# Expert weights of a mixture-of-experts layer kept in fp32, multiplied in halves and quarters of the TensorE array

## The chip, the cores and the metric

The kernel runs on one core of one Trainium2 chip. The metric is device time in microseconds for one launch. TensorE does the matrix products, VectorE (DVE), ScalarE (ACT) and GpSimd (POOL) the elementwise work, SyncE (SP) issues the transfers.

## The reference, cut to what matters

A two-layer decoder trunk on 272 tokens of width 1024 (16 of them learned ones that are dropped at the end). Each layer mixes tokens with three branches; layer 0 then has a dense SwiGLU, layer 1 the expert layer that the change touches:

```python
logits = xt @ router_w                       # 256 tokens x 8 experts
top_v, top_i = lax.top_k(logits, 2)
comb = sum(one_hot(top_i) * softmax(top_v))  # weight of each expert for each token
for e in range(8):                           # D_FF_EXPERT = 3584
    out = out + comb[:, e:e+1] * (silu(xt @ wg[e]) * (xt @ wu[e])) @ wd[e]
```

All tensors are float32.

## The kernel before, in words

All weights lie in one array `w` of units of 128 x 2048 float32 (1 MB). The dense part takes 109 units, each expert 42. `Stream` loads the units in order into a ring of tiles (names `raw`, and later `xh`, `xl`, `lt`, `mg`, which the dense part has freed). A tile that is released lets SP issue the next load. `Stream.block(512)` hands out the next 512 columns; an expert has 168 such blocks of 128 x 512 (256 KB each): for each of 7 slices `j` of the hidden width, 8 blocks for the gate and 8 for the up product (`gate_up`), then 8 blocks for the product with the down weights of slice `j-1` (`down`).

The tokens of an expert are gathered into slots with one-hot matrices (`Run.gather`). The experts are worked on in the order q = 0 to 7, of the kinds `KINDS = "BSBSBBBS"`, ordered by load so that an S expert has at most 64 tokens and a B expert at most 96 (`SMALL`, `CAP`). A general version for fuller experts stands behind a condition (`tc.If`) and isn't executed with these inputs.

A B expert works on split weights. `Stream.high` copies half a unit to fp32r on ACT (`whi`, L152), `Stream.low` subtracts on DVE (`wlo`, L165), and `mm3` makes three fp32r products of 512 columns for each block (L275 to L277), with 96 slots as the stationary operand and the activations split too (`xgh`, `xgl`, and `eh`, `el` for the hidden values). An S expert takes the weights as they are, in fp32 (`st.whole`): for each block two products of 256 columns, with the 64 slots in the left and in the right 64 columns of the array (L1309, L1328), which write partitions 0 to 63 and 64 to 127 of one PSUM bank. The trace shows each fp32 product as two MATMULs.

Hidden values are brought to the other layout by TensorE transposes (`transpose_h` L1208, `transpose_small` L1214), and each expert's results go back to the tokens by products with the one-hot matrix (`scatter` L1231, `scatter_small` L1238) and an accumulation on DVE. Much of that is put into `pending`, from which `gate_up` takes one piece before k = 3 and k = 6 of each product. A helper `keep_clock` multiplies junk in halves and in quarters of the array during the routing (L306).

Experts are gathered in groups, (0), (1, 2), (3, 4), (5, 6, 7); at the end of a group (`turnover`) the next one is gathered, and `slot_rms` (L1113, L1114) brings the norm's scale to the slots. Expert 0 runs alone: behind it all pending work is done at once, all engines load a flag, and experts 1 to 7 stand inside `tc.If(full <= CAP)`.

Of the kernel before, what the change touches and what calls it, by code (L numbers as in the profile page):

```python
# [16 lines left out]
P = 128  # L17
# [17 lines left out]
PASSES = -(-SEQ // CAP)  # L35
SMALL = 64

# [10 lines left out]
UNITS = DENSE_UNITS + NEXP * EXP_UNITS  # L48

# [30 lines left out]
class Stream:  # L80
# [5 lines left out]
    def __init__(self, nc, w, raws, hl, nhl, first, last):  # L86
        self.nc, self.w = nc, w
        self.ring = list(raws)
        self.at = 0
        self.hl, self.nhl = hl, nhl  # L90
        self.next_dma, self.end = first, last
        self.next_hi = self.next_lo = 2 * first
        self.cur = 2 * first - 1
        self.units, self.halves = {}, {}
        self.pos, self.first = 0, 2 * first
        self.whole, self.src = set(), lambda u: w[u]
        self.used, self.oldest, self.apart = set(), first, set()
# [45 lines left out]
    def high(self):  # L143
# [12 lines left out]
    def low(self):  # L156
        h = self.next_lo
        if h // 2 in self.whole:
            self.next_lo += 1
            if h % 2:  # L160
                del self.units[h // 2]
            return
# [15 lines left out]
    def advance(self):  # L178

        if self.cur < self.pos // HALF + self.first:  # L180
            self.halves.pop(self.cur, None)
            if self.cur % 2 and self.cur // 2 in self.whole:
                self.release(self.cur // 2)
# [19 lines left out]
def _build(ctx, tc, nc, A, out, dbg):  # L203
    V, S, G, PE = nc.vector, nc.scalar, nc.gpsimd, nc.tensor
    w = A["w"]
    NRAW, NHL, NRAWB, NRAWC = 6, 3, 4, 1
# [693 lines left out]
    def before_last():  # L900
# [11 lines left out]
        slots2 = me.tile([P, 2 * SMALL], F32, name="slots2")  # L912
# [7 lines left out]
        G.iota(slots2, pattern=[[0, 2], [1, SMALL]], base=1, channel_multiplier=0, allow_small_or_imprecise_dtypes=True)  # L920
        G.iota(index, pattern=[[1, NEXP]], base=0, channel_multiplier=0, allow_small_or_imprecise_dtypes=True)
        for k_, v_ in (("tri", tri), ("oneb", oneb), ("lower", lower), ("slots", slots), ("slots2", slots2),
# [59 lines left out]
    tri, oneb, lower, slots, slots2 = em["tri"], em["oneb"], em["lower"], em["slots"], em["slots2"]  # L982
# [24 lines left out]
    es = me.tile([P, 512], F32, name="es")  # L1007
# [27 lines left out]
    tiles = {}  # L1035

    def kept(pool, shape, dt, nm):

        if nm not in tiles:
            tiles[nm] = pool.tile(shape, dt, name=nm)  # L1040
        return tiles[nm]

    class Run:


        def __init__(self, kinds, groups, pos, comb):
            self.kinds, self.groups, self.pos, self.comb = kinds, groups, pos, comb
            self.x, self.oh, self.at, self.turn = {}, {}, {}, 0
# [5 lines left out]
        def first(self, i):  # L1054

            return SMALL if any(self.small(q) for q in self.groups[i]) else 0

        def onehot(self, i):
            oh = [kept(me, [P, 2 * SMALL + 2 * CAP], F32R, f"oh{t}") for t in range(2)]
            o = 0  # L1060
            for q in sorted(self.groups[i], key=lambda q: not self.small(q)):
                n = 2 * SMALL if self.small(q) else CAP
                self.at[q] = o
                for t in range(2):
                    V.tensor_scalar(oh[t][:, o:o + n], slots2 if self.small(q) else slots, self.pos[:, t, q:q + 1], None,
                                    op0=OP.is_equal)
                self.oh[q] = [oh[t][:, o:o + n] for t in range(2)]
                o += n
            self.all = [oh[t][:, self.first(i):o] for t in range(2)]

        def gather(self, i, c2, tag):

            if c2 == 0:
                for q in self.groups[i]:
                    if self.small(q):
                        self.x[q] = kept(mo, [P, KD, SMALL], F32, "xn")
                    else:
                        self.turn = 1 - self.turn
                        self.x[q] = [kept(mo, [P, KD, CAP], F32R, f"{n}{self.turn}") for n in ("xgh", "xgl")]
            p = bank(tag)  # L1080
            n = self.all[0].shape[1]
            for c in range(2):
                cc = 2 * c2 + c
                for k, src in enumerate((em["nh"], em["nl"])):
                    for t in range(2):
                        PE.matmul(p[:, c * n:(c + 1) * n], lhsT=src[:, t, cc * P:(cc + 1) * P], rhs=self.all[t],
                                  start=k + t == 0, stop=k + t == 2)

            def part(q, c):
                o = c * n + (0 if self.small(q) else self.at[q] - self.first(i))  # L1090
                return p[:, o:o + (SMALL if self.small(q) else CAP)], pp("g_ffn", 1, 1, 2 * c2 + c)

            for q in self.groups[i]:
                for c in range(2):
                    src, g = part(q, c)
                    if self.small(q):
                        V.tensor_scalar(self.x[q][:, 2 * c2 + c, :], src, g, None, op0=OP.mult)
                    else:
                        S.activation(self.x[q][0][:, 2 * c2 + c, :], src, AF.Copy, scale=g)
            for q in self.groups[i]:  # L1100
                if not self.small(q):
                    for c in range(2):
                        src, g = part(q, c)
                        h, l = (x[:, 2 * c2 + c, :] for x in self.x[q])
                        V.scalar_tensor_tensor(l, src, g, h.bitcast(F32), op0=OP.mult, op1=OP.subtract)

        def slot_rms(self, i):

            p = bank("o")
            for q in self.groups[i]:  # L1110
                n = self.oh[q][0].shape[1]
                for t in range(2):
                    PE.matmul(p[:n, q:q + 1], lhsT=self.oh[q][t].bitcast(F32), rhs=ssq[:, t:t + 1], start=t == 0, stop=t == 1)  # L1113
                V.tensor_copy(rs[:n, q:q + 1], p[:n, q:q + 1])  # L1114

    def again_by_tokens(t, d):
# [5 lines left out]
        split_to(em["nh"][:, t, cs], em["nl"][:, t, cs], acc[t][d])  # L1122
# [4 lines left out]
    rs = one([P, NEXP], F32, "rs")  # L1127
# [3 lines left out]
    V.tensor_reduce(cnt, pp_[:, 16:24], axis=AX.X, op=OP.max)  # L1131
# [23 lines left out]
    S.activation(rs[:, :2], ssq, AF.Silu)  # L1155
# [12 lines left out]
    flag = one([P, 1], F32, "flag")  # L1168
    flagi = one([P, 1], I32, "flagi")
    sq = [P, NEXP, NEXP]  # L1170

    def rank_steps():

        a, b = pair_
        V.tensor_scalar(cn[:, 0:1], cn[:, 0:1], 2.0 * SEQ, None, op0=OP.add)
        cj, ce = cn[:, None, :].to_broadcast(sq), cn[:, :, None].to_broadcast(sq)
# [18 lines left out]
        V.tensor_tensor(b[:, 0], a[:, 1], cn, op=OP.mult)  # L1195
        V.tensor_reduce(flag, b[:, 0], axis=AX.X, op=OP.add)
        V.scalar_tensor_tensor(flag, flag, float(CAP - SMALL), cnt, op0=OP.add, op1=OP.max)
        V.tensor_copy(flagi, flag)
# [3 lines left out]
    def room(name):  # L1202
        return mo.tile([P, 512], F32R, name=name, bufs=2)

    def transpose_h(h, dst):
        p = bank("acc")
        for b in range(4):
            PE.transpose(p[:, b * CAP:(b + 1) * CAP], h[:CAP, b * P:(b + 1) * P], ident[:CAP, :CAP])  # L1208
        split_to(*dst, p[:, :4 * CAP])

    def transpose_small(h, dst):
        p = bank("acc")
        for b in range(2):
            PE.transpose(p[:, b * P:(b + 1) * P], h[:, b * P:(b + 1) * P], ident)  # L1214
        V.tensor_copy(dst, p[:, :256])  # L1215

    def slots_by_token(run, q, oht):
        p = bank("o")
        n = run.oh[q][0].shape[1]
        for t in range(2):  # L1220
            PE.transpose(p[:n, t * P:(t + 1) * P], run.oh[q][t].bitcast(F32), ident)
        S.activation(oht[:n], p[:n, :256], AF.Copy)

    def split_y(ys, y):
        ys += [room(n) for n in ("eh", "el")]
        split_to(*(x[:CAP] for x in ys), y[:CAP])

    def scatter(run, q, oht, ys, t, d, tag):
        p = bank(tag)
        for i in range(2):  # L1230
            PE.matmul(p, lhsT=oht[:CAP, t * P:(t + 1) * P], rhs=ys[i][:CAP], start=i == 0, stop=i == 1)  # L1231
        V.scalar_tensor_tensor(acc[t][d], p, run.comb[:, t, q:q + 1], acc[t][d], op0=OP.mult, op1=OP.add)

    def scatter_small(run, q, oht, y, t, g, ds, tag):

        p = bank(tag)
        r = slice(g * SMALL, (g + 1) * SMALL)
        PE.matmul(p[:, :256 * len(ds)], lhsT=oht[r, t * P:(t + 1) * P].bitcast(F32),  # L1238
                  rhs=y[r, ds[0] * 256:(ds[-1] + 1) * 256], start=True, stop=True)
        for i, d in enumerate(ds):  # L1240
            o = acc[t][d][:, g * 256:(g + 1) * 256]
            V.scalar_tensor_tensor(o, p[:, i * 256:(i + 1) * 256], run.comb[:, t, q:q + 1], o, op0=OP.mult, op1=OP.add)
# [12 lines left out]
    def square_sums(d):  # L1255

        fin = XG["fin"]
        for t in range(2):
            scratch = me.tile([P, 512], F32, name="es")
# [22 lines left out]
    def experts(st, run, qs):  # L1282
# [3 lines left out]
        def hidden(q, j):  # L1286

            h = hid.get((q, j), ())
            if len(h) == 1:
                if run.small(q):  # L1290
                    h.append(room("eh")[:, :256].bitcast(F32))
                    transpose_small(h[0], h[1])
                else:
                    h += [room(n)[:, :4 * CAP] for n in ("eh", "el")]
                    transpose_h(h[0], h[1:])

        def gate_up(q, j, last):
            gu = []
            for m in range(2):
                a = bank(("acc", "s")[m])  # L1300
                for k in range(KD):
# [4 lines left out]
                    wh, wl = st.block(512)  # L1306
                    if run.small(q):
                        for g in range(2):
                            PE.matmul(a[g * SMALL:(g + 1) * SMALL, :256], lhsT=run.x[q][:, k, :],  # L1309
# [281 lines left out]
```

## Time and profile before

| | us |
|---|---|
| median of 3 runs (lowest, highest) | 1668.86 (1667.41, 1669.78) |
| the profiled execution, its own time | 1667.66 |
| span of its trace, first to last instruction | 1665.9 |
| first matmul of the experts, from the span's start | 758.06 |
| matmuls of B expert 0 | 758.1 to 883.8 |
| S expert 1 | 896.8 to 975.0 |
| B expert 2 | 975.0 to 1110.9 |
| S expert 3 | 1110.9 to 1191.0 |
| B experts 4, 5 and 6 | 1191.0 to 1568.4 |
| S expert 7 and the end | 1568.4 to 1665.9 |

The profile is of one execution. The matmul rows give the modelled time of a MATMUL from its start to its last result; matmuls follow each other sooner than that, so prices are read from start to start. Weight loads into the array have rows of their own (PEld).

### The profile page before, as it was taken

The numbers are of one execution on the slowest core, as the hardware profiler recorded it, in microseconds if no ns is written. First come the engines' busy times: TensorE is split into PE (matmuls) and PEld (weight loads), VectorE is DVE, ScalarE is ACT, GpSimd is POOL, SyncE is SP. The second block draws the span as 40 slices with busy tenths as digits, with TensorE's granted clock in tenths as the row PEclk, the third lists the DMA queues.
The fourth block names the chain that finished last, engine by engine and source line by source line (L and its number), as shares of the span: only waits on it lengthen the run. The fifth ranks groups of instructions, "written<-read, shape, count | busy, mean of one in ns | idle before, by whom it ended". The sixth has DMA issues, their size and how long they took to land.

```text
span 1665.9 us, 27719 instructions
## 1 busy us (share of the span) xinstructions
PE 1631.3 (98%) x10760; PEld 1319.1 (79%) x10760; DVE 1093.5 (66%) x1521; ACT 906.3 (54%) x1227; POOL 136.4 (8%) x205
## 2 busy tenths in 40 slices
PE   8999999999999999999998999999999999999997
PEld 8999999999999999997765656666666677777664
DVE  5667676555566576769993058950489898998602
ACT  5545656444444457557871048730377677778401
POOL 3301242000011002510000000000000000000000
PEclk9999999999999999998998999999999999999998
DMA  7333454544544336577895999999999999999994
GB/s 295 127 127 137 163 180 154 180 175 177 177 167 150 127 136 258 191 279 293 320 370 224 418 419 420 419 381 417 419 420 419 400 352 377 355 366 365 354 420 201
DMA packets 66235, 471.85 MB, mean 283 GB/s; under 512 B 7344, under 2 KB 7472, under 8 KB 9520
## 3 DMA queue, kind: packets, MB, share of 16 engines
q1 hardware_dynamic: 65952, 469.86, 72.5%
q8 instruction: 86, 1.41, 0.3%
q14 instruction: 53, 0.43, 0.1%
q10 hardware_dynamic: 144, 0.15, 0.0%
HBM read 468.93 MB, written 1.05 MB: 282 GB/s over the span
## 4 chain that ended last, share of the span: by engine, by line
PE 92%; DMA 3%; DVE 2%; POOL 1%; ACT 1%; issue 0%; SPq 0%; ACTq 0%; DVEq 0%; POOLq 0%
PE acc L275 12%; PE acc L276 12%; PE acc L277 12%; PE t L276 6%; PE s L275 6%; PE s L276 6%; PE s L277 6%; PE t L275 6%; PE t L277 6%; PE acc L1309 4%; PE s L1309 4%; PE t L1328 3%; DMA raw<-w 2%; DMA xh<-w 1%; PE o L1231 1%; PE s L516 1%
## 5 line engine op out<-in xcount | busy, mean ns | idle before, releaser
L152 ACT ACTIVATE whi<-raw 128x1024 fp32r<-128x1024 f32 x524 | 552.3, 1058 | 250.2 <-issue 57.3
L165 DVE TENSOR_TENSOR wlo<-raw,whi 128x1024 fp32r<-128x1024 f32 x524 | 630.6, 1230 | 49.6 <-PE acc L277 14.3
L275 PE MATMUL acc<-xh,whi 128*128 128x272 f32 (+1 forms) x864 | 252.6, 292 | 0.0
L277 PE MATMUL acc<-xh,wlo 128*128 128x272 f32 (+1 forms) x864 | 247.8, 287 | 0.8 <-DVE wlo L165 0.8
L276 PE MATMUL acc<-xl,whi 128*128 128x272 f32 (+1 forms) x864 | 247.4, 286 | 0.0
L275 PEld LDWEIGHTS acc<-xh,whi 128*128 128x128 f32 x864 | 162.6, 188 | 1.6 <-issue 0.9
L277 PEld LDWEIGHTS acc<-xh,wlo 128*128 128x128 f32 x864 | 162.7, 188 | 1.0 <-DVE wlo L165 1.0
L276 PEld LDWEIGHTS acc<-xl,whi 128*128 128x128 f32 x864 | 162.9, 189 | 0.1
L1317 ACT ACTIVATE es<-acc,rs 96x512 f32<-96x512 f32 (+1 forms) x56 | 33.3, 594 | 180.6 <-PE acc L1214 157.9
L276 PE MATMUL t<-wlo,eh 128*96 128x512 f32 x280 | 112.6, 402 | 1.5 <-DVE wlo L165 1.0
L275 PE MATMUL acc<-whi,xgh 128*96 128x512 f32 x280 | 112.2, 401 | 0.3 <-ACT whi L152 0.3
L275 PE MATMUL s<-whi,xgh 128*96 128x512 f32 x280 | 112.2, 401 | 0.0
L275 PE MATMUL t<-whi,eh 128*96 128x512 f32 x280 | 112.2, 401 | 0.0
L276 PE MATMUL acc<-wlo,xgh 128*96 128x512 f32 x280 | 111.1, 397 | 0.8 <-DVE wlo L165 0.8
L277 PE MATMUL acc<-whi,xgl 128*96 128x512 f32 x280 | 110.8, 396 | 0.0
L277 PE MATMUL t<-whi,el 128*96 128x512 f32 x280 | 110.6, 395 | 0.0
L276 PE MATMUL s<-wlo,xgh 128*96 128x512 f32 x280 | 110.4, 394 | 0.0
L277 PE MATMUL s<-whi,xgl 128*96 128x512 f32 x280 | 109.9, 392 | 0.0
L1318 DVE SCALAR_TENSOR_TENSOR es<-s,rs,es 96x512 f32<-96x512 f32 (+1 forms) x56 | 36.3, 647 | 75.0 <-PE s L1309 67.2
L1215 DVE COPY eh<-acc 128x256 f32<-128x256 f32 x21 | 8.9, 425 | 116.1 <-PE acc L1214 116.1
L276 PEld LDWEIGHTS t<-wlo,eh 128*96 128x96 f32 x280 | 45.8, 164 | 23.5 <-DVE wlo L165 5.2
L275 PEld LDWEIGHTS acc<-whi,xgh 128*96 128x96 f32 x280 | 45.6, 163 | 23.2 <-issue 3.0
(449 smaller groups left out, 3272.5 us busy)
## 6 DMA issues: line engine op xcount, KB each, us to landing
raw<-w SPq DMA_DIRECT2D x352, 1024.0 KB, 6.9
xh<-w SPq DMA_DIRECT2D x22, 1024.0 KB, 10.9
xl<-w SPq DMA_DIRECT2D x22, 1024.0 KB, 12.1
lt<-w SPq DMA_DIRECT2D x22, 1024.0 KB, 14.1
mg<-w SPq DMA_DIRECT2D x22, 1024.0 KB, 14.3
raw<-w SPq DMA_DIRECT2D x6, 512.0 KB, 8.2
hT<-hT SPq DMA_DIRECT2D x4, 272.0 KB, 7.5
lw<-lruw SPq DMA_DIRECT2D x2, 512.0 KB, 8.1
```

The source lines that it names most:

```text
L152: self.nc.scalar.activation(hi, src, AF.Copy)
L165: self.nc.vector.tensor_tensor(lo, src, hi.bitcast(F32), op=OP.subtract)
L275: PE.matmul(ps, lhsT=wh, rhs=xh, start=start, stop=False)
L276: PE.matmul(ps, lhsT=wh, rhs=xl, start=False, stop=False)
L277: PE.matmul(ps, lhsT=wl, rhs=xh, start=False, stop=stop)
L516: PE.matmul(s[:nq, c0:c0 + nk], lhsT=q[:, t0 - q0:t0 - q0 + nq], rhs=ks, start=True, stop=True)
L1215: V.tensor_copy(dst, p[:, :256])
L1231: PE.matmul(p, lhsT=oht[:CAP, t * P:(t + 1) * P], rhs=ys[i][:CAP], start=i == 0, stop=i == 1)
L1309: PE.matmul(a[g * SMALL:(g + 1) * SMALL, :256], lhsT=run.x[q][:, k, :], rhs=wh[:, g * 256:(g + 1) * 256], start=k == 0, stop=k == KD - 1)
L1317: S.activation(s[:n, :c], gu[0][:n, :c], AF.Silu, scale=r)
L1318: V.scalar_tensor_tensor(s[:n, :c], gu[1][:n, :c], r, s[:n, :c], op0=OP.mult, op1=OP.mult)
L1328: PE.matmul(a[g * SMALL:(g + 1) * SMALL, :256], lhsT=h[0][:, k % 2 * P + k // 2 * SMALL:k % 2 * P + (k // 2 + 1) * SMALL], rhs=wh[:, g * 2 ...
```

## The change

All eight experts take the fp32 weights as they lie in the ring (`WHOLE` holds every unit of the experts), so `high` and `low` do nothing there. For each block, `products` makes the two half-array products on the first 64 slots as an S expert does, and for a B expert four more, each of 32 slots on 128 columns in one quarter of the array's columns. The layout of the hidden values, their transposes (now three of 128 x 128 for a B expert) and the scatter follow from that: `split_y` splits the results into fp32r pieces laid out block-diagonally in zeroed tiles `YD`, and `scatter` multiplies them with one-hot matrices that repeat the slots (`by_slot`). The norm's scale is applied to the tokens in `again_by_tokens`, except for expert 0, where `by_slot` makes the scales of its slots; `slot_rms` is gone. All experts run in one sequence, with the conditions for fuller experts behind them. The ring has one tile more (`NRAWC` 2).

```diff
+WHOLE = set(range(DENSE_UNITS, UNITS))
...
-        if u in self.whole:
+        if u in WHOLE:
             self.halves[h] = (src, None)
...
-    NRAW, NHL, NRAWB, NRAWC = 6, 3, 4, 1
+    NRAW, NHL, NRAWB, NRAWC = 6, 3, 4, 2
...
+    def products(a, x, y, w, start, stop):
+        for g in range(2):
+            PE.matmul(a[g * SMALL:(g + 1) * SMALL, :256], lhsT=x, rhs=w[:, g * 256:(g + 1) * 256], start=start,
+                      stop=stop and y is None)
+        if y is not None:
+            for r in range(4):
+                PE.matmul(a[r * MORE:(r + 1) * MORE, 256:384], lhsT=y, rhs=w[:, r * P:(r + 1) * P], start=False, stop=stop,
+                          tile_position=(0, r * MORE))
...
+    YD = [[spare_half(n).rearrange("p (d c) -> p d c", d=2) for n in ns] for ns in (("wlo", "wlo"), ("wlo", "whi"))]
...
+    def split_y(run, q, d, a):
+        for (hi, lo), n, c0, cw in ((YD[0], SMALL, 0, 256), (YD[1], MORE, 256, P))[:1 if run.small(q) else 2]:
+            for i in range(P // n):
+                r, c = slice(i * n, (i + 1) * n), slice(i * cw, (i + 1) * cw)
+                split_to(hi[r, d, c], lo[r, d, c], a[r, c0:c0 + cw])
...
+    def scatter(run, q, oht, t, d, tag):
         p = bank(tag)
+        n = 1 if run.small(q) else 2
+        for i in range(n):
+            for k, y in enumerate(YD[i]):
+                PE.matmul(p, lhsT=oht[:, (2 * i + t) * P:(2 * i + t + 1) * P], rhs=y[:, d, :], start=i + k == 0, stop=i + k == n)
...
-                    wh, wl = st.block(512)
-                    if run.small(q):
-                        for g in range(2):
-                            PE.matmul(a[g * SMALL:(g + 1) * SMALL, :256], lhsT=run.x[q][:, k, :],
-                                      rhs=wh[:, g * 256:(g + 1) * 256], start=k == 0, stop=k == KD - 1)
-                    else:
-                        mm3(a[:CAP], *(x[:, k, :] for x in run.x[q]), wh, wl, k == 0, k == KD - 1)
+                    x = run.x[q][:, k, :]
+                    products(a, x[:, :SMALL], x[:, SMALL:] if n > SMALL else None, st.block(512)[0], k == 0, k == KD - 1)
...
             if turnover:
-                for c2 in range(2 if alone else 4):
+                for c2 in range(4):
                     run.gather(i + 1, c2, ("s", "acc")[c2 % 2])
-                if not alone:
-                    run.slot_rms(i + 1)
...
-    full = load(flagi)
-    with tc.If(full <= CAP):
-        experts(st, fast, range(1, NEXP))
+    experts(st, fast, True)
```

## Rows read from the trace of the kernel before

**Rows 1.** The page, in 40 slices of 41.6 us: granted TensorE clock, and transfers.

```profile
PEclk9999999999999999998998999999999999999998
GB/s 295 127 127 137 163 180 154 180 175 177 177 167 150 127 136 258 191 279 293 320 370 224 418 419 420 419 381 417 419 420 419 400 352 377 355 366 365 354 420 201
```

**Rows 2.** Stages (S; B): us busy PE, PEld, DVE, ACT, POOL; clock; DMA; GB/s.

```profile
897.00:975.00 78.00, 77.75 (x688) 49.99 (x687) 6.95 (x16) 4.79 (x10) 0.00 (x0) 0.99 0.96 395
1317.00:1443.00 126.00, 125.04 (x556) 87.99 (x557) 111.31 (x111) 95.84 (x101) 0.00 (x0) 0.99 0.94 362
```

**Rows 3.** Loads of a unit by SP, and SP's longest wait.

```profile
raw<-w SPq DMA_DIRECT2D x352, 1024.0 KB, 6.9
SPq L124 <- DVE wlo L165: 834.8, 226, 11.8
```

**Rows 4.** Timeline of TensorE, B expert: start us, us, what; eight blocks, then transposes.

```profile
771.55 0.40 PE L275 MATMUL acc<-whi,xgh 128*96 128x512 f32 x1
...
777.12 0.49 PE L1208 MATMUL acc<-ident,es 96*128 96x96 f32 x4
777.40 0.45 PE L275 MATMUL s<-whi,xgh 128*96 128x512 f32 x1
```

**Rows 5.** Timeline of TensorE, S expert: eight blocks, two transposes, eight blocks.

```profile
927.09 3.62 PE L1309 MATMUL acc<-raw,xn 128*64 128x256 f32 x32
930.64 0.44 PE L1214 MATMUL acc<-ident,es 128*128 128x128 f32 x2
931.01 3.67 PE L1309 MATMUL s<-raw,xn 128*64 128x256 f32 x32
```

**Rows 6.** Timeline of TensorE near the end: one block in halves between half-height products.

```profile
1651.18 0.65 PE L1328 MATMUL t<-raw,eh 128*64 128x256 f32 x4
1651.77 0.70 PE L1238 MATMUL acc<-eh,oht 64*128 64x256 f32 x2
1652.39 0.44 PE L1328 MATMUL t<-raw,eh 128*64 128x256 f32 x2
```

**Rows 7.** Timeline of TensorE, junk products in quarters, and what follows them.

```profile
750.64 1.07 PE L306 MATMUL s<-nh 128*32 128x256 f32 x16
751.64 0.43 PE L1086 MATMUL acc<-oh,nh 128*128 128x96 f32 x2
```

**Rows 8.** That line's own matmuls, ns min/median/max.

```profile
L306 PE MATMUL s<-nh x32: 379/379/431, 746.7 to 751.3; 128*64 128x256 f32 x16, 128*32 128x256 f32 x16
```

**Rows 9.** Timeline of TensorE: a piece of scatter, S's amid B, B's amid S, B's amid B.

```profile
980.40 1.12 PE L1238 MATMUL o<-eh,oht 64*128 64x512 f32 x2
981.45 0.47 PE L275 MATMUL acc<-whi,xgh 128*96 128x512 f32 x1
...
1112.37 0.50 PE L1231 MATMUL o<-eh,oht 96*128 96x512 f32 x1
...
1113.03 0.44 PE L1309 MATMUL acc<-raw,xn 128*64 128x256 f32 x2
...
1330.75 0.40 PE L1231 MATMUL o<-eh,oht 96*128 96x512 f32 x1
...
1331.22 0.40 PE L275 MATMUL acc<-whi,xgh 128*96 128x512 f32 x1
```

**Rows 10.** Timeline of TensorE around the first, second and third turnover.

```profile
883.84 0.35 PE L1086 MATMUL s<-oh,nh 128*128 128x160 f32 x2
...
896.85 2.95 PE L1309 MATMUL acc<-mg,xn 128*64 128x256 f32 x16
899.62 1.91 PE L1309 MATMUL acc<-raw,xn 128*64 128x256 f32 x16
...
1103.29 0.50 PE L1113 MATMUL o<-ssq,oh 128*96 128x1 f32 x4 [3.70 <-DVE rs L1114]
...
1317.71 0.50 PE L1113 MATMUL o<-ssq,oh 128*96 128x1 f32 x4 [3.36 <-DVE rs L1114]
```

**Rows 11.** The last 7 us of the first turnover: busy us, clock, DMA.

```profile
890.00:897.00 7.00, 4.33 (x10) 1.76 (x10) 3.01 (x5) 0.00 (x0) 0.00 (x0) 0.50 0.00 0
```

More of the change, by code (lines that the diff above doesn't have):

```diff
@@ L1033, in _build, with spare_half @@
     V.scalar_tensor_tensor(pos, pp_[:, :16].rearrange("p (t e) -> p t e", t=2), 1.0, sel, op0=OP.add, op1=OP.mult)
[L1035 to L1041, printed above, removed]
+    def spare_half(name):
+        return hlp.tile([P, HALF], F32R, name=name, bufs=NHL + (name == "whi"))
     class Run:
@@ L1093, in gather @@
[L1093 to L1105, printed above, removed]
@@ L1109, in slot_rms @@
             p = bank("o")
[L1110 to L1111 removed]
+            for i in range(w // P):
                 for t in range(2):
[L1113 to L1114 removed]
+                    PE.transpose(p[:, (2 * i + t) * P:(2 * i + t + 1) * P], ohd[t][:, i * P:(i + 1) * P], ident)
+            S.activation(oht[:, :2 * w], p[:, :2 * w], AF.Copy)
@@ L1116, in again_by_tokens @@
+            if scales:
+                p = bank("o")
+                for i in range(2):
+                    for t in range(2):
+                        PE.matmul(p[:, i:i + 1], lhsT=ohd[t][:, i * P:(i + 1) * P], rhs=ssq[:, t:t + 1], start=t == 0,
+                                  stop=t == 1)
+                V.tensor_copy(rs, p[:, :2])
     def again_by_tokens(t, d):
@@ L1199, in rank_steps @@
+        V.tensor_reduce(cnt, cnr, axis=AX.X, op=OP.max)
+        V.tensor_scalar(cnt, cnt, 0.0, None, op0=OP.max)
         V.tensor_copy(cnti, cnt)
         yield
[L1202 to L1215, printed above, removed]
@@ L1280, in _build, with experts @@
     pending = []
-    def experts(st, run, qs):
+    def experts(st, run, first):
         hid, dn_, oht = {}, {}, {}
@@ L1334, in results @@
[L1334 to L1355 removed]
+            h = hid[q, j][1]
@@ new lines, in down, with results @@
+            o = k % 2 * P + k // 2 * SMALL
+            products(dn_[q][d], h[:, o:o + SMALL], None if run.small(q) else h[:, 256 + k * MORE:256 + (k + 1) * MORE],
+                     st.block(512)[0], j == k == 0, j == FJ - 1 and k == 3)
+        def results(q, d, final):
+            a = dn_[q][d]
+            if d == 0 or final:
+                split_y(run, q, d, a)
+            else:
+                pending.append(lambda: split_y(run, q, d, a))
+            pending.extend([lambda t=t: scatter(run, q, oht[q], t, d, "acc" if final else "o") for t in range(2)])
@@ L1363, in experts @@
             turnover = q == run.groups[i][-1] and not final
-            ys = []
             last = None
+            oht[q] = mo.tile([P, 4 * P], F32R, name="oht")
+            if q == 0:
+                pending.append(lambda: run.by_slot(0, oht[0], first))
+                if first:
+                    ranking = rank_steps()
+                    pending.extend([lambda: next(ranking)] * 6)
             for j in range(FJ):
@@ L1401, in experts @@
                     down(q, FJ - 1, d, k)
-                results(q, d, ys, final)
-            if alone:
-                for c2 in range(2, 4):
-                    run.gather(i + 1, c2, ("s", "acc")[c2 % 2])
-                run.slot_rms(i + 1)
-                while pending:
-                    pending.pop(0)()
-        if NEXP - 1 in qs:
-            while pending:
-                pending.pop(0)()
-            result()
+                results(q, d, final)
+        while pending:
+            pending.pop(0)()
+        result()
     SP = mybir.EngineType.SP
+    pending = []
     order = {}
@@ L1420, in load_order @@
                                       skip_runtime_bounds_check_because="the index of an expert")
-    ring = st.ring[st.at:] + st.ring[:st.at]
-    def stays(i):
-        def tile_of_unit():
-            if i not in tiles:
-                tiles[i] = ring[i]()
-            return tiles[i]
-        return tile_of_unit
-    st.ring, st.at = [stays(i) for i in range(len(ring))], 0
     by_unit = w[DENSE_UNITS:UNITS].rearrange("(e u) p f -> u e p f", e=NEXP)
```

223 lines of the change are left out of this document (89 added, 134 removed).

## The prediction

> **What bounds the kernel now.** I read the page's slices first, then the stages, then TensorE's timeline inside each kind of expert, and last what the loads wait for. The slices show the clock near full and the transfers rising to some 420 GB/s only in the expert part [rows 1]. Read across the stages, TensorE is busy for nearly all of an S expert (77.75 of 78 us) and of a B stretch (125.04 of 126), while the transfers fall to 362 GB/s in the long B run [rows 2]; SP's longest wait, 834.8 us, is for the split weights that free a ring tile [rows 3]. So loads are ahead, and the B experts are bound by TensorE or the split that feeds it. The timeline decides: in B, eight blocks run from 771.55 to 777.12, 0.696 us a block, 24 fp32r products 0.232 us apart without holes [rows 4]. Loads could go faster: a block is a quarter of a 1024 KB unit, 0.62 us at 419 GB/s [rows 1, 3]. ACT and DVE are each busy for over three quarters of a B stretch [rows 2] but keep up. What the change does to TensorE's time per B block therefore decides; there are 5 x 168 = 840 such blocks.
>
> **Price of the new B block.** Three parts, each from start to start.
>
> Halves. An S expert's 32 MATMULs, 16 pairs, last 3.62 us, and a MATMUL's own modelled time is 0.38 [rows 5, 8]: (3.62 - 0.38) / 15 = 0.216 us a pair, two pairs a block, 0.432 us. Quarters. Junk products of 256 columns in quarters: 16 MATMULs last 1.07 us, so the fours too start about 0.23 us apart, (1.07 - 0.38) / 3 [rows 7]: four quarters run together. With 128 columns I take half of 0.216, 0.108 us for each of two passes. If that were all, a block would take 0.432 + 0.216 = 0.648 us, and the change would win 840 x 0.048 = 40 us.
>
> The change of arrangement. The last pair of halves before the transposes starts at 927.09 + 3.62 - 0.38 = 930.33 and is streamed by 930.55, but the full-array transposes start at 930.64: 0.09 us in which nothing streams. Back in halves the same 32 MATMULs take 3.67 instead of 3.62, since the first loads of weights are not hidden: 0.05 more [rows 5]. Between fp32r products and transposes that both use the whole array there is no such hole: the transposes start 0.232 us after the product ahead of them, as any next product does [rows 4]. So it is neither the type nor the instruction, but the way the array is divided. It isn't only full against divided: near the end one block in halves stands between products of half height, and takes 1651.77 - 1651.18 = 0.59 us instead of 0.432; on the way back the half-height pass that starts at 1651.77 + 0.70 - 0.38 = 1652.09 is streamed by 1652.31 and the halves start at 1652.39 [rows 6], 0.08 later. In quarters, four passes from 750.64 to the next full-array product at 751.64 take 1.00 us against 4 x 0.216 = 0.864: 0.14 for loads and drain [rows 7].
>
> The new B block goes halves, quarters, halves, so it pays twice. Halves: 0.432 + 0.05 + 0.10 = 0.58 (the row has 0.59). Quarters: 2 x 0.108 + 0.14 = 0.355. Together 0.935 us instead of 0.696, that is 840 x 0.239 = 201 us more. No row shows halves against quarters themselves. Bounds: with no drain between them 0.648 (a gain, the rival below); with the drain but the first loads hidden, 0.05 and some 0.03 less, 0.86; with one more unhidden load in each half of the block, 0.08 more, 1.01. I take 0.935, because every change of division in the rows pays, divided against divided too [rows 5 to 7].
>
> The Trainium skill (TensorEngine Tiling (Array Packing), Key Properties) says that a change of the tiling mode, not a mere change of tile, drains TensorE. By it the halves and quarters drain as well and the sum stays at +201 us; read as no rule for two column divisions, it would be -40 us. The holes in the rows agree with it as far as they go.
>
> **The rest, part by part.** Hidden values of a B expert: now 777.12 to 777.40, and 0.05 for the next product, whose modelled time is 0.45 instead of 0.40, 0.33 us [rows 4]; after it three transposes, two of which take 931.01 - 930.64 = 0.37 with a drain [rows 5], so 0.48. 35 times 0.15: +5 us.
>
> Scatter. A B piece costs 1331.22 - 1330.75 = 0.47 us amid B and 1113.03 - 1112.37 = 0.66, with 0.14 for drain and reload 0.80, amid S [rows 9]. Before, experts 2 and 6 have four pieces each amid S, 4 and 5 amid B: 8 x 0.80 + 8 x 0.47 = 10. After, a B piece has four products, two more at 0.233: 1.27 amid S, and 1.13 amid B (there a change of division is paid anyway): 12 x 1.27 + 8 x 1.13 = 24, with expert 0's counted. +14 us. S pieces amid B: now 981.45 - 980.40 = 1.05, with 0.09 of drain ahead and 0.07 of late start behind (0.47 instead of 0.40), eight times [rows 9], 9.7; after, two fp32r products, 0.66: 5.3. -4 us.
>
> Turnovers. The first one keeps TensorE from 883.84 to 896.85 with scatter and scales one after the other at a clock of 0.50 at its end, and the next 16 products take 2.95 instead of 1.91 [rows 10, 11]. Of these 14.0 us only the gather, some 1.75 (an estimate: 16 MATMULs at about 0.11, as for the transposes of the same 128 columns of weights), stays: -12. The two later ones lose 3.70 and 3.36 us to the scales' copies, queued on DVE behind the gather's copies, with two rounds of it and a slower clock after it, about 6.5 each [rows 10]: -13. In the new sequence the scatter is pending work and the scales are gone from the turnovers.
>
> The split (ACT, DVE) goes; it is hidden but for refills at the starts of B stretches, for which I allow -3. `by_slot` has two more transposes and its drain, +2. `split_y` does six small copies and six subtractions for a B expert where S products follow quickly, +3 for three such places. POOL's zeroing of `YD` has 120 us until expert 0's results. The longer condition at the end follows the last output transfers. The tail keeps its shape: two copies and two subtractions more ahead of fewer products, nothing counted. The load side is covered: an S expert eats 42 units in 78 us while 31 arrive [rows 2, 3], and the ring of 16 tiles is full after a B expert slower than its loads (42 x 2.5 = 105 us).
>
> Sum: 201 + 5 + 14 - 4 - 12 - 13 - 3 + 2 + 3 = +193 us on the profiled execution's 1667.66: 1861. The median of the runs is 1.2 above that execution; I forecast **1861 us**, 11.5% slower.
>
> **Rivals.**
> A, the forecast: each block drains twice. 0.79.
> B, other side: halves and quarters share the columns' division well enough that nothing drains between them. Against it all holes in rows 5 to 7; for it only that this pair isn't in the trace. Then -40 for the blocks instead of +201, 1620, and as a B expert (168 x 0.648 and some 9, 118 us) is then hardly slower than its loads, the ring isn't full when S experts start: 10 us of waiting, 1630 us. It decides if the loss is under 0.048 us a block. 0.10.
> C, weight loads don't hide: each B block has twelve loads, and quarters of 128 columns leave half the time for the next pass's. For it: loads behind a change show (0.05). Against: pairs in steady state come at 0.216 us, loads hidden. With 0.08 a block more, +64: 1925 us. 0.04. The Trainium skill (TensorE: Matmul & The Clock Gate, Part 3, The mechanism) lets loads pass running matmuls only where the row groups differ, and here they are the same rows; the steady pairs disagree with it.
> D, supply of instructions: 12 MATMULs and 12 loads a block instead of 3 and 3. If S's steady pace, four MATMULs in 0.432 us, were a ceiling, 1.296 a block, +303: 2164 us. Against it 16 MATMULs in 1.07 us [rows 7]. 0.03.
> E, the clock: only 0.648 of 0.935 us stream, and the clock did fall to 0.50 in a stretch with idle gaps [rows 11]. There TensorE did 10 MATMULs in 7 us; here 12 in one. If it fell, passes double: 0.65 a block more, +540: 2400 us. 0.04.
>
> **How the numbers follow.** A's own bounds are 0.86 and about 0.98 a block, with the other terms' few us: 1795 to 1900. The range takes in C: 1795 to 1925, which leaves out B, D, E: 0.17. Changes under 0.2% can't be told from none. Faster is B, 0.10; slower A, C, D and E, 0.90, of which I give 0.01 to a partial drain that just eats the gain, and so to no change.
>
> **What would show it.** In the changed trace: halves 0.58 and quarters 0.355 from start to start in each B block; a hole of about 0.09 us and loads that begin with their matmul at each change; B experts of 165 to 172 us and S experts of 80 to 83; transfers near 260 GB/s in B; clock near full; no wait on split weights; turnovers without holes of 3 us. B blocks of 0.65 us would make the forecast wrong, and clocks under 0.9 or blocks over 1.0 would make it too low.

## The result, and the profile after

The changed kernel takes 1867.34 us (median of 4 runs, 1866.46 to 1869.48), the kernel before 1668.79 (1667.41 to 1669.78). The ratio is 1.1192, 95% interval 1.1173 to 1.1212: 198.6 us slower, against 193 in the forecast. The profiled execution has a span of 1864.7 us.

The page of the kernel after: the busy time of the engines, and TensorE's granted clock in 40 slices, as in [rows 1].

```profile
PE 1836.3 (98%) x18303; PEld 1209.6 (65%) x18303; DVE 618.7 (33%) x1120; ACT 464.2 (25%) x811; POOL 140.3 (8%) x210
PEclk9999999999999999899999999999999999999998
```

Stages of the kernel after, with the columns of [rows 2]: S expert 1, then B expert 5.

```profile
927.80:1009.90 82.10, 82.10 (x710) 51.54 (x708) 12.31 (x30) 5.92 (x17) 0.00 (x0) 1.00 0.99 402
1427.90:1594.00 166.10, 166.10 (x2063) 64.95 (x2059) 15.23 (x32) 7.69 (x21) 0.00 (x0) 1.00 0.76 267
```

DVE and ACT are nearly idle in B now, 15.23 and 7.69 us of 166; the transfers have sunk to 267 GB/s, because SP waits 142 of these 166 us for ring tiles that TensorE has yet to read; TensorE is busy without a gap at full clock. And yet the B expert takes 166.1 us where the B experts before took some 126. So the time is inside TensorE's own sequence. Its timeline in the kernel after, in the manner of [rows 4]: transposes in expert 0, its gather at the first turnover, its last blocks, the start of S expert 1 with a piece of expert 0's scatter.

```profile
912.30 0.55 PE L1287 MATMUL acc<-ident,es 128*128 128x128 f32 x3
912.78 0.65 PE L1209 MATMUL t<-raw,whi 128*64 128x256 f32 x4
...
916.53 0.46 PE L1085 MATMUL s<-oh,nh 128*128 128x160 f32 x2
...
920.27 0.65 PE L1209 MATMUL t<-raw,whi 128*64 128x256 f32 x4
...
924.02 0.65 PE L1209 MATMUL t<-xh,whi 128*64 128x256 f32 x4
924.60 0.43 PE L1213 MATMUL t<-xh,whi 128*32 128x128 f32 x8
924.96 0.65 PE L1209 MATMUL t<-xh,whi 128*64 128x256 f32 x4
...
927.77 1.51 PE L1209 MATMUL acc<-xl,xg 128*64 128x256 f32 x12
929.22 0.96 PE L1234 MATMUL o<-wlo,oht 128*128 128x512 f32 x3
...
930.34 0.65 PE L1209 MATMUL acc<-xl,xg 128*64 128x256 f32 x4
```

Read from start to start: halves 924.60 - 924.02 = 0.58, quarters 924.96 - 924.60 = 0.36, a block 0.94 us; over the more than 700 blocks that nothing interrupts the median is 0.938. A scatter piece lasts 930.34 - 929.22 = 1.12 in the S expert and as long in B expert 5 (from 1443.28 to 1444.40), the three transposes 0.48. The 3 us holes at the turnovers [rows 10] are gone: the gather runs from 916.53 to 920.27 amid the last blocks of expert 0, and the next expert's products follow at once.

### The profile page after: what moved, and what is told of

It reads as the page before. It is cut to its first block, busy times and chain, and to the rows that moved or that the text cites. A ratio compares the mean times of both kernels' runs of the same rounds, so it can differ in the third digit from the quotient of the medians.

```text
span 1864.7 us, 41097 instructions
## 1 busy us (share of the span) xinstructions
PE 1836.3 (98%) x18303; PEld 1209.6 (65%) x18303; DVE 618.7 (33%) x1120; ACT 464.2 (25%) x811; POOL 140.3 (8%) x210
## 4 chain that ended last, share of the span: by engine, by line
PE 96%; POOL 1%; DVE 1%; ACT 1%; DMA 0%; issue 0%; SPq 0%; ACTq 0%; DVEq 0%; POOLq 0%
PE acc L1209 13%; PE s L1209 13%; PE t L1209 13%; PE acc L277 7%; PE acc L279 7%; PE acc L278 7%; PE acc L1213 5%; PE s L1213 5%; PE t L1213 5%; PE s L277 2%; PE s L278 2%; PE s L279 2%; PE t L278 2%; PE t L277 2%; PE t L279 2%; PE o L1234 2%
## 5 line engine op out<-in xcount | busy, mean ns | idle before, releaser
L167 DVE TENSOR_TENSOR wlo<-raw,whi 128x1024 fp32r<-128x1024 f32 x218 | 272.0, 1248 | 35.7 <-PE acc L279 13.8
L154 ACT ACTIVATE whi<-raw 128x1024 fp32r<-128x1024 f32 x218 | 229.3, 1055 | 155.1 <-issue 51.4
L1209 PE MATMUL acc<-raw,xg 128*64 128x256 f32 x1328 | 196.6, 398 | 4.3 <-issue 4.3
L1209 PE MATMUL s<-raw,xg 128*64 128x256 f32 x1344 | 196.1, 396 | 0.0
L1209 PE MATMUL t<-raw,whi 128*64 128x256 f32 x1328 | 190.0, 394 | 0.0
L1209 PEld LDWEIGHTS t<-raw,whi 128*64 128x64 f32 x1328 | 77.5, 135 | 58.5 <-issue 39.1
L1209 PEld LDWEIGHTS s<-raw,xg 128*64 128x64 f32 x1344 | 76.2, 135 | 60.3 <-issue 44.0
L1213 PE MATMUL acc<-raw,xg 128*32 128x128 f32 x1696 | 91.0, 287 | 0.0
L1213 PE MATMUL s<-raw,xg 128*32 128x128 f32 x1696 | 90.3, 285 | 0.0
L1213 PE MATMUL t<-raw,whi 128*32 128x128 f32 x1568 | 83.5, 285 | 0.0
```

The source lines that it names most:

```text
L154: self.nc.scalar.activation(hi, src, AF.Copy)
L167: self.nc.vector.tensor_tensor(lo, src, hi.bitcast(F32), op=OP.subtract)
L1209: PE.matmul(a[g * SMALL:(g + 1) * SMALL, :256], lhsT=x, rhs=w[:, g * 256:(g + 1) * 256], start=start, stop=stop and y is None)
L1213: PE.matmul(a[r * MORE:(r + 1) * MORE, 256:384], lhsT=y, rhs=w[:, r * P:(r + 1) * P], start=False, stop=stop, tile_position=(0, r * MORE))
```

## Experiments: is it the change of arrangement?

All experiments start from the kernel after, unless another is named. The theory was that each change between halves and quarters costs TensorE a drain and unhidden loads. The rival was that the twelve MATMULs of a block cost what they cost, however they are ordered.

**Half as many changes (e1_turned).** Every second block does its quarters first, so two blocks go halves, quarters, quarters, halves.

```diff
-        products(..., k == 0, k == KD - 1)
+        products(..., k == 0, k == KD - 1, k % 2)      # turned: quarters first
```

> The changed kernel, with the same products in another order: every second block of a B expert takes its quarters first and its halves last, so that neighbouring blocks meet in the same division of the array. Half of the changes between halves and quarters go; the number of MATMULs, of weight loads and of streamed columns stays. Theory drain (each change of the array's division costs about 0.145 us of drain and unhidden loads): a B block falls from 0.938 to about 0.79 us on average, 840 x 0.145 = 122 us less, about 1745 us. Rival count (the extra 0.29 us of a block come from its twelve MATMULs and twelve loads): the block stays at 0.94 us and the time at about 1867 us.

Measured 1755.24 us in one run, 112 below after. TensorE's timeline of this kernel:

```profile
1100.54 1.08 PE L1210 MATMUL t<-raw,whi 128*64 128x256 f32 x8
1101.56 0.64 PE L1215 MATMUL t<-raw,whi 128*32 128x128 f32 x16
1102.13 0.65 PE L1210 MATMUL t<-raw,whi 128*64 128x256 f32 x4
```

Two blocks take 1.02 us of halves and 0.57 of quarters, 0.795 a block in these rows and 0.794 in the median, with one change each instead of two. The same instructions in another order: the count is not the price.

**No change at all (e2_halves).** The 32 further slots run as a second half-array pair. The results of those slots are left out of what the kernel computes; the loads and the MATMULs are the cost that counts.

```diff
-            for r in range(4):
-                PE.matmul(a[r * MORE:(r + 1) * MORE, 256:384], lhsT=y, rhs=w[:, r * P:(r + 1) * P], ...)
+            for g in range(2):
+                PE.matmul(a[g * SMALL:(g + 1) * SMALL, 256:512], lhsT=y, rhs=w[:, g * 256:(g + 1) * 256], ...)
```

> The changed kernel with the quarter products replaced: the 32 more slots ride in a second pair of half-array products with 64 columns of weights (32 of them slots that the first pair has too), so a B block streams a third more (0.864 instead of 0.648 us) but never changes the array's division. The later steps still read the quarters' layout, so the results of the 32 more slots are left out of the output. Theory drain: a block takes 0.864 us, 840 x 0.074 = 62 us less than the changed kernel, about 1805 us, although more is streamed. Rival count: 8 MATMULs and loads instead of 12, 0.864 + 0.29 x 8 / 12 = 1.06 us a block, about 1967 us. A rival by which quarter products are slow in themselves (0.357 us for what should stream in 0.216) would also give about 1805 us; the order experiments tell that one apart.

Measured 1812.57 us in one run, 54.8 below after, although it streams 0.216 us more in each block. TensorE's timeline:

```profile
1099.86 0.60 PE L1213 MATMUL t<-raw,whi 128*64 128x256 f32 x4
1100.29 0.60 PE L1209 MATMUL t<-raw,whi 128*64 128x256 f32 x4
```

Every 0.43 us two pairs, with no hole: 0.864 a block. 840 times (0.938 - 0.864) is 62 us; 7 less came.

**Two changes in eight blocks (e3_groups).** Eight blocks in halves, then their eight in quarters (four and four in the second layer); the ring's tiles are held until the quarters have read them.

```diff
+                    halves(a, x[:, :SMALL], wt, k == 0, ...)
+                    rest.append(lambda ...: quarters(a, x[:, SMALL:], wt, k == KD - 1))
...
+                finish()        # the quarters of these eight, then their tiles are released
```

> The changed kernel with the halves and quarters of a B expert done in groups: eight blocks in halves, then the same eight in quarters, for the gate and for the up product, and four and four in the product with the down weights; ring tiles are given back after the group, and the pending pieces are taken between groups. All products and loads as before, outputs complete. Theory drain: two changes for eight blocks, 0.648 + 0.29 / 8 = 0.684 us a block, and 0.648 + 0.29 / 4 = 0.72 us in the down part; per B expert 112 x 0.684 + 56 x 0.72 = 117 instead of 157.6 us, 203 us less in all, about 1664 us, the same as the kernel before within 1%. Rival count, and the rival that quarter products are slow in themselves: about 1867 us.

Measured 1670.38 us (1669.04 to 1671.29), ratio to before 1.0016 [1.0006, 1.0025]: 197 us came back. TensorE's timeline:

```profile
1004.48 3.67 PE L1218 MATMUL acc<-raw,xg 128*64 128x256 f32 x32
1008.09 1.95 PE L1222 MATMUL acc<-raw,xg 128*32 128x128 f32 x64
1009.97 0.55 PE L1296 MATMUL acc<-ident,es 128*128 128x128 f32 x3
```

Eight blocks take 1009.97 - 1004.48 = 5.49 us, 0.686 each. The halves take 3.61, that is 8 x 0.432 + 0.15; the quarters 1.88, that is 8 x 0.216 + 0.15. With 2, 1 and 1/4 changes a block the three kernels give 0.938, 0.794 and 0.686: a line with a slope of some 0.145 us, which meets 0.65 at none. That is the 0.648 of bare streaming that the prediction had computed, so what the kernel after pays above it, 0.29 us a block, is its two changes.

## Experiments: the rest of the change

**The turnovers alone (e5_turnover).** The kernel before, with one sequence of experts, the pending scatter and the scale on the tokens, and the split weights kept. The general version for fuller experts is left out.

```diff
-            alone = len(qs) == 1
...
-            if alone:
-                for c2 in range(2, 4):
-                    run.gather(i + 1, c2, ("s", "acc")[c2 % 2])
-                run.slot_rms(i + 1)
-                while pending:
-                    pending.pop(0)()
...
+    experts(st, fast, range(NEXP))
```

> The kernel before, with split weights as it had them, and of the change only this: experts in one sequence without a condition amid them, expert 0's results as pending work, and the norm's scale put on the tokens so that the turnovers have no scales to bring to slots. The general version for fuller experts is left out. By the terms of the prediction (12 us at the first turnover, 13 at the other two) the kernel before becomes 25 us faster, about 1644 us. Rival: the loads or the split of weights take over what the holes covered, and little is gained, 1660 to 1669 us.

Measured 1646.60 us (1645.94 to 1649.01), ratio 0.9881 [0.9864, 0.9897], beside 1667.56 for before on that chip: 21 us gained. Two rows of it, TensorE's first product after a gather's copies, and the last ACT work (span 1644.2):

```profile
880.75 0.47 PE L276 MATMUL t<-wlo,eh 128*96 128x512 f32 x1 [2.08 <-DVE wlo L165]
...
1638.86 1.32 ACT L1277 ACTIVATE raw<-raw,rfin 128x512 f32<-128x512 f32 x2
```

The last ACT work of the kernel before (span 1665.9):

```profile
1657.72 1.32 ACT L1275 ACTIVATE raw<-raw,rfin 128x512 f32<-128x512 f32 x2
```

Two things are mixed in the 21 us. There is no condition at the end, so only 1644.23 - 1640.18 = 4.05 us follow the last work, where before has 1665.88 - 1659.04 = 6.84, from its own last ACT work: 2.8 us of the gain. And each turnover still waits some 2 us (2.08 in the row, 2.14 and 1.69 in the other two) for weights that DVE splits behind the gather's copies. The kernel after has no split. So the turnover part is worth 21 - 2.8 = 18 here and, by an estimate that adds these three waits, some 24 where nothing is split: the forecast had 25.

**Two uncounted costs.** After's trace shows two idle stretches that the prediction had at nothing. First, the start of expert 0: POOL, then DVE, then TensorE in the kernel after.

```profile
750.75 2.56 POOL L997 TENSOR_TENSOR hacc<-nh,nl 128x512 f32<-128x512 f32 x2 [3.44 <-DVE ssq L1144]
753.47 2.73 POOL L1221 MEMSET wlo<- 128x1024 f32 x3
756.14 0.95 POOL L1221 MEMSET whi<- 128x1024 f32 x1
...
750.78 6.34 DVE L1146 TENSOR_SCALAR L<-L,ssq 128x8 f32<-128x8 f32 x2
...
758.18 1.12 PE L1209 MATMUL acc<-raw,xg 128*64 128x256 f32 x4 [4.32 <-issue]
```

Two scalings of 8 columns last 6.34 us on DVE, until POOL ends (757.1), and TensorE stands for 4.32 us: the copies of the gathered tokens on DVE and ACT are queued behind what follows from that scaling. In the kernel before this same pair took 2.78. `YD`'s zeroing on POOL was suspected. The pair in the kernel before, and the times of the two in the kernel after (ns: shortest, median, longest):

```profile
752.35 2.78 DVE L1146 TENSOR_SCALAR L<-L,ssq 128x8 f32<-128x8 f32 x2
```

```profile
L1146 DVE TENSOR_SCALAR L<-L,ssq x2: 1298/3213/5128, 750.8 to 752.0; 128x8 f32<-128x8 f32 x2
```

*Moved on POOL (e4_zero_later).* The zeroing becomes a piece of `pending`, still on POOL.

```diff
+    def zeros():
         for pair in YD: ...
                 G.memset(y.bitcast(F32), 0.0)
...
+                    pending.append(zeros)
```

> The changed kernel with POOL's zeroing of the four scatter tiles moved from the routing into the pending work of expert 0. In the changed kernel's trace two small DVE operations of the routing (128x8) take 6.34 us together while POOL adds and zeroes, and TensorE then has a hole of 4.32 us before the first expert product and runs its first blocks at half clock. Theory: DVE is held up by POOL's zeroing, so without it those two take some 2.8 us as in the kernel before, the hole shrinks to below 1 us and the slow clock mostly goes: about 7 us less, 1860 us. Rival (the hole comes from the evacuation of the gather, which waits for TensorE or ACT): no difference, 1867 us.

Measured 1867.58 us, ratio 1.1199 [1.118, 1.1218]: no difference, but also no test. POOL's queue has nothing in front of the zeroing that waits for TensorE, so it ran at 753.55, as in the kernel after, and DVE's pair took 6.32. A later place in the program's text isn't a later time on an engine that is idle.

*On VectorE (e7_zero_dve).* The same piece of `pending`, on DVE, whose queue is in order with expert 0's work.

```diff
-                G.memset(y.bitcast(F32), 0.0)
+                V.memset(y.bitcast(F32), 0.0)      # as a piece of pending
```

> The kernel after, with the zeroing of the four YD tiles given to VectorE as one item of the work that waits for places among expert 0's blocks; ScalarE, POOL and the products are as they were. If it is POOL's zeroing beside the routing that held VectorE's 128x8 scaling for 6.34 us: that scaling takes some 2.8 us as before, TensorE's hole ahead of expert 0 is under 1.5 us instead of 4.32, its first blocks need not run at half clock, and the whole takes 1858 to 1863 us. If it is POOL's adds of 2.56 us that held it: the scaling stays over 3 us longer than those adds, the hole stays, 1867 us. If the start of expert 0 is set by the copies of the gathered tokens anyway: the scaling is short, the hole stays, 1867 us.

Measured 1863.51 us (1862.88 to 1864.64), 3.8 below after; 1.1177 [1.1161, 1.1192] of before. Timeline of DVE, then TensorE:

```profile
751.00 2.79 DVE L1146 TENSOR_SCALAR L<-L,ssq 128x8 f32<-128x8 f32 x2
...
754.85 1.12 PE L1209 MATMUL acc<-raw,xg 128*64 128x256 f32 x4 [0.77 <-issue]
```

The scaling is short, the hole is 0.77 us, expert 0 starts 3.3 us sooner. POOL's adds and its small zeroing (2.8 us) hold DVE's pair too, for as long as they last. The Trainium skill (SBUF — State Buffer, SBUF: two separate sides) says that DVE and GpSimd share one pair of ports to SBUF, as an exclusive lock: of a GpSimd instruction and a DVE instruction that uses both ports, the one that starts first has the pair for its whole instruction, and the other is fully blocked. The rows agree that DVE stands for as long as POOL works: 6.34 us with 6.3 us of POOL's work beside it, 2.79 with 2.8. They show a longer hold than one instruction's: in the kernel after the second scaling starts at 752.0, with POOL's second add, and lasts 5.13 us, through that add and the twelve memsets, eight of one column and four of 1024, that follow it without a gap.

*The end (e9_nested).* In after, the last ACT work (row below, first) ends at 1853.96 and the span at 1864.7: 10.7 us, against 6.8 before. Here the second condition is moved into the body of the first.

```diff
-    for r in range(PASSES):
-        with tc.If(left > CAP * r):
+    def one_pass(r):
+        with tc.If(left > CAP * r):
             ...
+            one_pass(r + 1)
```

> The kernel after, with the second condition at the end placed inside the body of the first (what runs when the first fails, as here, is one branch instead of two). If the two branches, one behind the other, make the 11.0 us between the last work and the end: some 6.5 to 7 us remain and the time is 1863 us. If a branch costs the same whatever its length and the end waits for the output transfers: no difference, 1867 us.

Measured 1863.58 us (1862.94 to 1863.93), ratio 1.1176 [1.116, 1.1191], 3.8 below after. The last ACT work of after, and that of this kernel (span 1861.9):

```profile
1852.64 1.32 ACT L1268 ACTIVATE raw<-raw,rfin 128x512 f32<-128x512 f32 x2
```

```profile
1853.88 1.32 ACT L1268 ACTIVATE raw<-raw,rfin 128x512 f32<-128x512 f32 x2
```

From the end of that work 1861.9 - 1855.2 = 6.7 us remain. With no condition it was 4.1 (e5_turnover), with one 6.7 to 6.8 (this kernel and before), with two 10.7: each condition that fails costs some 3 to 4 us behind the last output, although nothing inside it runs. What the engines do in that time was not looked into.

## A version that beats both

**Sixteen blocks to a change (e6_wide).** Gate and up product together, sixteen blocks in halves and then sixteen in quarters, eight and eight in the second layer, with the nested conditions. The zeroing stays on POOL, as in e4_zero_later.

```diff
+                for m in range(2):
+                    for k in range(KD):
+                        halves(gu[m], x[:, :SMALL], wt, k == 0, False)
+                        rest.append(lambda ...: quarters(a, x[:, SMALL:], wt, k == KD - 1))
+                hidden(*last)
+                finish()
```

> The changed kernel with wider groups: the sixteen blocks of the gate and up product in halves, then the same sixteen in quarters, and the eight down blocks likewise, so four changes of division for 24 blocks; also POOL's zeroing later, and the two conditions behind the experts one inside the other, so that the engines branch once. Outputs complete. Theory drain: 0.648 + 0.58 / 24 = 0.672 us a block against 0.696 in the narrower groups, 840 x 0.024 = 20 us less than the 1670 us of those, 8 less for the zeroing and 3 for the second branch, 1640 us, faster than the kernel before by 1.7%. Rival: the loads or longer holding of ring tiles take over, 1655 to 1670 us.

Measured 1647.70 us (1646.99 to 1648.05), ratio 0.988 [0.9863, 0.9896]: faster than before, 8 us short of what was expected; 8 us had been expected of the zeroing, which in this form changes nothing (e4_zero_later). **With the zeroing on DVE (e8_wide_dve)**, the edit of e7_zero_dve on top of it:

> The kernel with 16 half-array blocks and then their 16 quarter-array blocks (8 and 8 in the second layer) and the nested conditions, 1647.7 us, and the zeroing on VectorE as in the kernel sent beside this one. If POOL's zeroing holds up the start: 1640 to 1644 us. If not: 1648 us. Were the saved time given back because the transfers, 418 GB/s in these stretches, are the bound: 1646 to 1648 us with the hole ahead of expert 0 gone.

Measured 1642.82 us (1641.83 to 1643.84), ratio 0.9853 [0.9836, 0.9869]: 24 us faster than before on that chip (1667.09). A sequence of sixteen blocks on its TensorE, and stages of it (an S stretch, B expert 5):

```profile
1309.73 3.67 PE L1218 MATMUL acc<-raw,xg 128*64 128x256 f32 x32
1313.24 1.90 PE L1218 MATMUL s<-raw,xg 128*64 128x256 f32 x16
1314.96 1.90 PE L1218 MATMUL s<-xh,xg 128*64 128x256 f32 x16
...
1318.24 1.96 PE L1222 MATMUL acc<-raw,xg 128*32 128x128 f32 x64
1320.02 1.06 PE L1222 MATMUL s<-raw,xg 128*32 128x128 f32 x32
1320.89 1.06 PE L1222 MATMUL s<-xh,xg 128*32 128x128 f32 x32
```

```profile
1090.00:1170.00 80.00, 79.01 (x683) 49.50 (x684) 12.06 (x28) 5.66 (x16) 0.00 (x0) 1.00 1.01 419
1301.00:1424.00 123.00, 122.52 (x2061) 88.09 (x2059) 15.04 (x32) 7.70 (x20) 0.00 (x0) 1.00 0.96 385
```

TensorE is still busy for nearly all of both, but the loads have come close: 419 GB/s in S, 385 in B, where after had 267.

**Whose gain is it?** The new turnovers alone gave 21 us (e5_turnover). So the two stand beside each other on one chip, both without the general version: sixteen blocks to a change with the zeroing on DVE (e10_wide_only), and split weights with the new turnovers, the kernel of e5_turnover once more (e11_split_again).

```diff
-    left = nc.values_load(cnti[0:1, 0:1], ...)
...
-    one_pass(0)
```

> The kernel with sixteen blocks to a change and the zeroing on VectorE (1642.8 us), with the general version for fuller experts left out, so that it stands on the same footing as the kernel beside it (before with only the new turnovers, split weights). If the conditions cost what the ends of the traces show: 6.66 - 4.1 = 2.6 us less, 1640 us. If unsplit weights in this order are worth something of their own beyond the turnovers: at least 5 us below the kernel beside it. If all its gain is that of the turnovers: the same time within 2 us, some 1645 us.

> The kernel before with only the new sequence and turnovers, split weights, the general version left out: as in its first run, 1646 to 1647 us, on the chip of the kernel beside it, for the difference of the two.

Measured 1639.73 us (1639.37 to 1640.47), ratio 0.9833 [0.982, 0.9847], and 1648.92 (1647.14 to 1651.97), 0.9889 [0.987, 0.9907]. The unsplit weights in this order win 9.2 us of their own, among them the waits for split weights at the turnovers, 6 us in e5_turnover's trace. A part of it may be the clock: the mean granted clock was 0.997 in e10's profiled run, 0.992 in e11's and 0.995 in that of e5_turnover, the same kernel as e11; against before on its own chip e5_turnover is 8.0 us behind e10 (0.9881 and 0.9833). The conditions are worth some 3 us: 1642.82 - 1639.73 = 3.1, and in the traces 6.7 us follow the last ACT work in e8 and 4.15 in e10. Of the 40 us that streaming without any change would win in the blocks, three quarters still go elsewhere: four changes are left in 24 blocks (35 x 4 x 0.145 = 20 us, an estimate), the scatter has become dearer, and the loads are near what they reach; these three were not separated by a run.

## Why the prediction was right, step by step

The forecast was 1861 us with a drain at each change; 1867.34 came, inside its range, for the reason given.

**The block** was forecast at 0.935 us, halves 0.58 and quarters 0.355; measured 0.938, 0.58 and 0.36. The price of a change was put together from full-array work next to divided work [rows 5 to 7], and held for halves against quarters, which no row had shown. The three orders with equal work settle it: 0.145 us a change. They change the division and the streamed columns (256 and 128) together; that it's the division, rows 6 say, where the halves and the products of half height both stream 256 columns and a block in halves still takes 0.59 us instead of 0.432. That it is 0.09 of drain and 0.05 of unhidden loads is the split that the prediction argued from rows 5; the experiments priced only the sum. The Trainium skill's rule (TensorEngine Tiling (Array Packing), Key Properties) that a change of mode drains agrees with e1 to e3, which show a price for each change between two divisions by columns, the reading that the prediction had left open; that the price is a drain, they don't show.

**The rivals.** B, no drain, fell with e1 to e3. C, loads that don't hide: between like products they do hide, since e2 has 0.216 us a pair and e3 0.216 a block of quarters. (Its 0.08 us a block are 840 x 0.08 = 67 us and not 64, so that its 1928 lay just outside the range.) D, a ceiling on instructions: in e3 the quarters run 64 MATMULs in 1.88 us, 0.029 apart, far below the 0.108 of that rival. E, the clock: 1.00 in the B stretch.

**What it would show** came so: B experts of 166.1 to 169.6 us (165 to 172 forecast), S experts 82.1 (80 to 83), 267 GB/s in B (260), no hole at the turnovers. Transposes 0.48 and scatter amid B 1.12 were forecast at 0.48 and 1.13. (The 31 units that were to arrive in an S expert, 78 us at 395 GB/s, are 29 of 1024 KB each; the ring of 16 tiles still covers the rest.)

**Sizes that were off.** The term of 25 us for the turnovers holds in sum by the estimate above (18 in e5_turnover, and the 6 us of its split waits). The gather in it was priced rightly: in the kernel before the second half of it, 16 MATMULs, stands in the hole from 883.84 [rows 10] to the row below, 1.75 us. After, all 32 run together in 3.74 us; the other 16 ran before as well, ahead of that hole.

```profile
885.59 0.54 PE L1113 MATMUL o<-ssq,oh 128*128 128x1 f32 x4
```

Two terms set to nothing cost some 3 to 4 us each: POOL's zeroing, for which the prediction asked only whether it would be done in time and not whom it would hold up meanwhile (e7_zero_dve, 3.3 us at the start of expert 0), and the second condition, which does not run beside the last output transfers but on after them (e9_nested, 4.0 us at the end). Both are 3.8 by the medians, and some 2 if each kernel is held against before on its own chip. With 3.8 for each the sum would be 193 + 7.6 = 200.6 us, and 198.6 came; the blocks' 0.003 us too little is 2.5 more. The 5 us that this is too high are spread over the small terms (refills, scatter, copies) and were not taken apart.

**Misses among the expectations.** e1, e2 and e3 ended 10, 8 and 6 us above theirs. For e2 the reason is likely that the scatter pieces and transposes, which in after fall on a change that is paid anyway, now bring changes of their own: some 11 to an expert, 55 x 0.145 = 8 us, an estimate from rows that was not tested. In e3 part of it can be seen: expert 0's `by_slot` waits 6.36 us for DVE with no other work between.

## What to carry to other kernels

Count the changes of the array's division, not only the columns that stream: here each cost 0.145 us. Order the work so that like products stand together: with two changes in sixteen blocks the unsplit weights were some 8 to 9 us faster than the split ones with the same turnovers, with two in each block some 200 us slower than the kernel before. And work on an engine that is idle isn't free: ask what its work holds up while it runs, and remember that a place later in the text doesn't delay an engine that has nothing to wait for.

## What the runs showed that had not been expected

Two scalings of 128 x 8 on DVE, where neighbours of 128 x 16 take 0.17 us, took 6.34 us while POOL added and zeroed, and 2.79 where it did little but add.

A condition that fails, around a large body, put 2.7 us behind the last work and a second one 3.9 more (4.1, 6.8 and 10.7 us in all); nesting took the second away.

How slowly expert 0's first blocks run isn't set by the hole ahead of them alone. The rows are windows with the columns of the stages above: two of after, then one each of e7_zero_dve, e8_wide_dve and e10_wide_only.

```profile
750.00:754.00 4.00, 3.86 (x36) 3.65 (x32) 3.96 (x5) 1.33 (x2) 3.25 (x11) 1.00 0.65 272
758.20:765.40 7.20, 6.51 (x45) 2.70 (x45) 2.04 (x10) 2.65 (x6) 0.00 (x0) 0.57 0.30 125
```

```profile
754.80:762.00 7.20, 6.46 (x44) 2.67 (x44) 2.12 (x10) 2.73 (x6) 0.00 (x0) 0.57 0.76 292
```

```profile
754.80:762.00 7.20, 7.20 (x56) 4.83 (x55) 1.79 (x9) 1.80 (x4) 0.00 (x0) 0.81 0.69 284
```

```profile
754.80:762.00 7.20, 6.90 (x64) 5.36 (x64) 2.13 (x10) 2.38 (x6) 0.00 (x0) 1.00 0.77 292
```

In all four TensorE was busy at clock 1.00 (2.4 GHz) up to the hole (the first row shows it for after; the same window has 1.00 in the other three). Behind it the granted clock is 0.57 over 7 us, near the lower level of 1.2 GHz, after 4.32 us of idling (after) and after 0.77 (e7_zero_dve) alike; but after holes of 0.76 and 0.77 us it is 0.81 in e8_wide_dve and 1.00 in e10_wide_only, where it didn't fall at all. So e7_zero_dve won the 3.3 us of its shorter hole and nothing of the clock; and a few us between two kernels here can be the clock's, as above between e10 and e11.
